# Five RMS-norm statistics taken off the matrix engine: turn, sum and spread through DRAM

## The chip, the cores and the metric

The kernel runs on one core of a Trainium2 chip. The metric is the device time of one execution in microseconds (us). The kernel before was timed three times: 2127.67, 2127.96 and 2129.14 us, median 2127.96 us. The trace is of one further, profiled execution.

## The reference

One layer of a streaming encoder on x of 1024 tokens by 1024 channels, all in f32: a SwiGLU feed-forward block, a token mixer (forgetting attention and top-k attention side by side) and a second SwiGLU block. Ahead of each stands an RMS norm over the channels, scaled and shifted by factors that come from a conditioning vector:

```python
def rms_norm(x, g):
    xf = x.astype(jnp.float32)
    y = xf * lax.rsqrt(jnp.mean(xf * xf, axis=-1, keepdims=True) + NORM_EPS)
    return (y * g.astype(jnp.float32)).astype(x.dtype)

def modulate(x, g, shift, scale):
    return rms_norm(x, g) * (1 + scale[:, None, :]) + shift[:, None, :]
...
h = modulate(x, norm_g[l, 0], mod[:, 0, 0], mod[:, 0, 1])
x = x + 0.5 * mod[:, 0, 2][:, None, :] * swiglu(h, ffn1_w1[l], ffn1_w3[l], ffn1_w2[l])
h = modulate(x, norm_g[l, 1], mod[:, 1, 0], mod[:, 1, 1])
y = hybrid_mixer(h, w_in[l], ...)
x = x + mod[:, 1, 2][:, None, :] * y
h = modulate(x, norm_g[l, 2], mod[:, 2, 0], mod[:, 2, 1])
x = x + 0.5 * mod[:, 2, 2][:, None, :] * swiglu(h, ffn2_w1[l], ffn2_w3[l], ffn2_w2[l])
```

Each token needs one number, the reciprocal root of the mean of its 1024 squares, and every channel of that token is multiplied by it.

## The kernel before

Activations lie transposed: x is eight tiles (one for each 128 channels, channel on the partition) by two halves of 512 tokens along the free side. A "half" below is 512 tokens. Three norms of two halves each make six norms. In the order of the kernel:

- the opening: the first half of the first norm. The work of the matrix engine (TensorE, PE in the profile) waits for it, and the change leaves it alone.
- norm A: the second half of the first norm, while PE works on products of the first half (`layer`, the second `sq = SquareSum`). Its factor goes into `Operands.second`, which scales the second half and forms the sums and differences that a Strassen-like scheme (`OPERANDS`, seven products for each pair of blocks) multiplies later.
- norm B: the first half of the second norm, inside the last passes of the first block's down-projection (`Down.run`, steps (5, 4) and (6, c)).
- norm C: the second half of the second norm, after the end of that down-projection. In between PE has only four projections of the first half, `first(0)` to `first(3)` (24 matmuls each, 128 x 432). Then the same projection runs over the second half, channel tile by channel tile, and needs norm C's factor for each of them (`norm_apply(k, 1, 1, ...)`, then `mm3` into four banks at once). Behind each `first(t)`, `natural` copies the bank to SBUF on ScalarE and stores it to DRAM (`d_na`).
- norm D: the first half of the third norm, inside `mixer_out`.
- norm E: the second half of the third norm, behind `mixer_out`, in the first steps of the second up-projection (`up_all`: twelve products of first-half operands come first, for three pairs of blocks).

Every norm has the same steps. `SquareSum.add` squares a tile on ScalarE (ACT) and adds it on VectorE (DVE) into one 128 x 512 accumulator, so that after eight tiles each partition holds a partial sum for each token. `norm_rms` sums over the partitions with four matmuls of the accumulator against a column of ones, one for each 128 tokens; `norm_root` turns the 128 x 4 result into reciprocal roots with twelve small DVE instructions; `norm_spread` puts them on all partitions with four matmuls of a broadcast column against the identity matrix. The result, `rb`, stays in a PSUM bank, from which DVE reads it as it scales the tiles (`Operands.scale`, `norm_apply`). Only norm E copies it from the bank to SBUF with ScalarE.

The order of instructions is planned before the kernel is built. `Plan` collects the tasks of a stage, and `flush` lists them for every engine by planned start time (`place`, `replay`, `dues`); the engines then run them in that order, each engine strictly in its own. All DMAs are issued from one queue, that of SyncE (SP), and one that has to wait holds back all behind it. The plan's price of a DMA is written in `place`:

```python
if e == "sync":
    self.wire = max(self.wire, s + 1.3) + t.bytes / 345e3
    end = self.wire + 1.7
```

Stages end at `nc.flush`. Opening, norm A and norm B lie in the first (up to the end of the first down-projection), norm C in the second, norms D and E in the last.

Of the kernel before, what the change touches and what calls it, by code (L numbers as in the profile page):

```python
# [10 lines left out]
F32 = mybir.dt.float32  # L11
# [15 lines left out]
H = 512  # L27
# [631 lines left out]
class SquareSum:  # L659


    def __init__(self, k, eng=None):
        self.k, self.acc, self.eng = k, None, eng or k.nc.gpsimd

    def add(self, x):
        nc = self.k.nc
        sq = t512(self.k, name="nsq" if self.acc else "nacc")
        nc.scalar.activation(sq, x, AF.Square)
        if self.acc:
            self.eng.tensor_add(self.acc, self.acc, sq)  # L670
        else:
            self.acc = sq

# [89 lines left out]
def t512(k, dt=F32, name="t", home="c"):  # L763

    p, tag, n = k.homes[home]
    return p.tile([128, H], dt, tag=tag, name=name, bufs=n)
# [1466 lines left out]
def layer(tc, xT, c, pos, ada_w, ada_b, ng, inv, w13a, w2a, w_a, w_f, w_q, w_g, fb, fg, dg, wbr, wout, w13b, w2b, out):  # L2233
    with ExitStack() as es:
# [45 lines left out]
        d_x = dram([8, 128, T], "d_x")  # L2280
        d_row = [[dram([1, H], f"d_row{i}{h}") for h in range(2)] for i in range(9)]
# [15 lines left out]
        with ExitStack() as ph:  # L2297
# [68 lines left out]
            def stats(j):  # L2366
                rms[j] = norm_rms(k, sq1[j].acc, rp, k.seeded if j == 0 else bank)

            def h0(cs):
                if cs[0] == 0:  # L2370
                    rms[0] = norm_spread(k, rms[0], bank)
                norm_apply(k, 1, 0, down.x, rms[0], cs)
# [28 lines left out]
            for i in range(8):  # L2401
                sq.add(x[i][0])
# [39 lines left out]
            rms[1] = norm_rms(k, sq.acc, rp, bank)  # L2442
            ops.rb[1] = norm_spread(k, rms[1], bank)
# [42 lines left out]
            nc.flush([t for r in down.x for t in r] + [t for r in wa for t in r] + k.hh[0] + k.hl[0] + [a.acc for a in sq1])  # L2486
# [17 lines left out]
            rb = norm_spread(k, rms[1], bank)  # L2504
# [133 lines left out]
        with ExitStack() as ph:  # L2638
# [25 lines left out]
            def stats(hf):  # L2664
                rms[hf] = norm_rms(k, sq[hf].acc, rp, bank)

            def spread(hf):
                ops.rb[hf] = norm_spread(k, rms[hf], bank)
                if hf:
                    t = t512(k, name="rb")  # L2670
                    nc.scalar.activation(t, ops.rb[hf], AF.Copy)
                    ops.rb[hf] = t
# [7 lines left out]
                10: [lambda: keep(0), lambda: spread(0)],  # L2680
                11: [lambda: more(0), pairs[0].load1], 12: [lambda: more(0), pairs[0].load2],
                13: [pairs[1].load1, lambda: pairs[0].sum32(nc.vector)], 14: [pairs[2].load1]}
            for n in range(9):
# [11 lines left out]
                   {1: [lambda: stats(1)], 3: [lambda: spread(1)], 4: [first1], 12: [next1], 14: [next1], 16: [next1],  # L2695
# [71 lines left out]
```

## Time and profile before

| | |
|---|---|
| median of three runs | 2127.96 us (2127.67 to 2129.14) |
| profiled execution, span from first to last instruction | 2126.6 us |
| PE matmuls busy | 2116.1 us (100% of the span) |
| PE weight loads busy | 1773.1 us (83%) |
| DVE busy | 1598.1 us (75%) |
| ACT busy | 1120.8 us (53%) |
| DMA, one queue | 216076 packets, 366.33 MB, 51.7% of 16 engines |

The profiled execution has no time of its own beside its span; the median of the runs is 1.4 us above that span, which is taken as what lies around it. Shares are over the whole span. Matmuls are pipelined, so each lasts longer in the trace (0.39 us) than the distance to the next (0.23 us), and the distance is what counts. "Idle before" and the name behind an arrow in a row tell what ended an engine's idle time.

### The profile page before, as it was taken

What the parts mean: (1) busy time and instruction counts of PE and PEld (TensorE: products, weight loads), DVE (VectorE), ACT (ScalarE), POOL (GpSimd) and SP (SyncE); (2) the same over time, 40 slices, a digit from 0 to 9 for tenths busy, and PEclk for the clock granted to TensorE, in tenths of its full rate; (3) what the DMA queues carried; (4) which work ended last, traced back from release to release, by engine and by line L of the source; (5) the groups of instructions that cost most, each with busy time, mean ns of one, the idle gap of its engine ahead of it and who ended that gap; (6) DMA issues with size and microseconds to landing.
All of it is one profiled execution on the core that took longest, in us unless ns stands there. A gap on an engine that the chain in (4) does not pass through costs nothing.

```text
span 2126.6 us, 31320 instructions
## 1 busy us (share of the span) xinstructions
PE 2116.1 (100%) x10632; PEld 1773.1 (83%) x10632; DVE 1598.1 (75%) x3079; ACT 1120.8 (53%) x2070; POOL 226.1 (11%) x231
## 2 busy tenths in 40 slices
PE   9999999999999999999999999999999999999999
PEld 7888888888888989998888777888888888888887
DVE  7987777879877399977886777698866755568665
ACT  4744444445456376886676777334543433334443
POOL 0001112200010110111442333000000000000000
PEclk9999999999999999999999999999999999999999
DMA  9446888899421444346453432896132533277521
GB/s 325 147 138 212 283 257 292 270 371 318 139 91 61 150 156 144 105 145 221 148 165 108 136 100 86 308 324 186 45 124 85 183 112 101 86 261 259 176 72 40
DMA packets 216237, 368.33 MB, mean 173 GB/s; under 512 B 29558, under 2 KB 67446, under 8 KB 216076
## 3 DMA queue, kind: packets, MB, share of 16 engines
q1 hardware_dynamic: 216076, 366.33, 51.7%
q8 instruction: 83, 1.36, 0.3%
q14 instruction: 78, 0.64, 0.1%
HBM read 268.99 MB, written 97.25 MB: 172 GB/s over the span
## 4 chain that ended last, share of the span: by engine, by line
PE 97%; DVE 2%; ACT 1%; issue 0%; DMA 0%; POOL 0%; SPq 0%; ACTq 0%; DVEq 0%; POOLq 0%
PE bs L606 38%; PE b L606 32%; PE pj L606 12%; PE py L606 8%; PE p L606 4%; PE pt L606 3%; DVE s L606 0%; DVE ptl L606 0%; DMA mraw<-in_ada_w 0%; ACT pth L606 0%; DVE qkv L606 0%; DVE pr L606 0%; ACT pr L606 0%; DVE qs L606 0%; DVE macc L606 0%
## 5 line engine op out<-in xcount | busy, mean ns | idle before, releaser
L606 PE MATMUL bs<-h,wh 128*128 128x512 f32 x1712 | 527.5, 390 | 1.1 <-ACT bs L606 0.7
L606 PEld LDWEIGHTS bs<-h,wh 128*128 128x128 f32 x1712 | 320.5, 188 | 70.0 <-ACT bs L606 1.6
L606 ACT ACTIVATE wh<-wr 128x512 fp32r<-128x512 f32 (+1 forms) x330 | 207.2, 638 | 295.4 <-PE bs L606 149.8
L606 PE MATMUL b<-h,wh 128*128 128x512 f32 x1072 | 332.5, 390 | 0.1
L606 PE MATMUL bs<-h,wl 128*128 128x512 f32 x856 | 331.6, 389 | 0.0
L606 DVE TENSOR_TENSOR wl<-wr,wh 128x512 fp32r<-128x512 f32 x306 | 211.4, 701 | 115.2 <-ACT wh L606 111.1
L606 PEld LDWEIGHTS b<-h,wh 128*128 128x128 f32 x1072 | 200.7, 188 | 43.2 <-ACT wh L606 0.5
L606 PE MATMUL b<-h,wl 128*128 128x512 f32 x536 | 208.3, 389 | 0.0
L606 PEld LDWEIGHTS bs<-h,wl 128*128 128x128 f32 x856 | 160.7, 188 | 33.6
L606 PE MATMUL pj<-wh,h 128*128 128x384 f32 (+1 forms) x768 | 178.4, 318 | 0.0
L606 ACT ACTIVATE wh<-a 128x512 fp32r<-128x512 f32 x132 | 83.4, 632 | 176.8 <-PE b L606 108.0
L606 DVE TENSOR_TENSOR wl<-a,wh 128x512 fp32r<-128x512 f32 x132 | 92.0, 698 | 81.9 <-ACT wh L606 79.7
L606 PE MATMUL b<-wh 128*128 128x512 f32 x360 | 138.7, 390 | 0.0
L606 PE MATMUL b<-wh,wl 128*128 128x512 f32 x352 | 136.7, 389 | 0.0
L606 PE MATMUL b<-wl,wh 128*128 128x512 f32 x352 | 136.7, 389 | 0.0
L606 PEld LDWEIGHTS pj<-wh,h 128*128 128x128 f32 x768 | 132.4, 189 | 0.3
L606 DVE TENSOR_TENSOR ptl<-pt,pth 128x512 fp32r<-128x512 f32 (+2 forms) x160 | 99.3, 634 | 41.0 <-ACT pth L606 40.2
L606 POOL TENSOR_SCALAR pr<-pr,mn 128x256 f32<-128x256 f32 (+7 forms) x128 | 102.1, 817 | 189.1 <-DVE mn L606 97.6
L606 PE MATMUL pj<-wl,h 128*128 128x384 f32 (+1 forms) x384 | 121.8, 318 | 0.0
L606 DVE TENSOR_TENSOR z<-bs,z 128x512 f32<-128x512 f32 x116 | 79.3, 687 | 56.3 <-PE bs L606 37.7
L606 PEld LDWEIGHTS b<-h,wl 128*128 128x128 f32 x536 | 100.6, 188 | 21.0
L606 ACT ACTIVATE pth<-pt 128x512 fp32r<-128x512 f32 (+2 forms) x160 | 87.0, 553 | 57.8 <-PE pt L606 56.2
(323 smaller groups left out, 4307.0 us busy)
## 6 DMA issues: line engine op xcount, KB each, us to landing
d_g<-z SPq DMA_DIRECT2D x154, 256.0 KB
g<-d_g SPq DMA_DIRECT2D x154, 256.0 KB
mraw<-in_ada_w SPq DMA_DIRECT2D x144, 256.0 KB
wr<-in_w13a SPq DMA_DIRECT2D x112, 256.0 KB
wr<-in_w13b SPq DMA_DIRECT2D x88, 256.0 KB
a<-in_w2a SPq DMA_DIRECT2D x44, 256.0 KB
a<-in_w2b SPq DMA_DIRECT2D x44, 256.0 KB
gw<-in_w_g SPq DMA_DIRECT2D x32, 256.0 KB
```

The costliest lines, as they stand in the source:

```text
L606: getattr(getattr(self.tc.nc, e), t.op)(*map(real, t.a), **{n: real(v) for n, v in t.kw.items()})
```

## The change

For norms A to E the partition sums and the spreading leave the matrix engine. The eighth addition of squares writes its result in another order of tokens (`turned`); DVE transposes it in blocks of 32 x 32 and sums groups of 32, which leaves, in each of four groups of 32 partitions, that group's partial sums of all 512 tokens. These 128 x 16 numbers are stored to DRAM (first transfer) and read back so that each partition has the four partial sums of four tokens (second transfer); DVE adds the four, and `norm_root` follows on 128 x 4 numbers as before. The roots are stored to DRAM as one row of 512 (third transfer) and read back to all 128 partitions as a 128 x 512 tile (fourth transfer). That tile in SBUF takes the place of the PSUM bank; norm E's copy on ScalarE goes. All four transfers are issued from SP. The accumulator tile and one more tile stay in use until then. The opening keeps its matmuls.

```diff
@@ class SquareSum
-    def add(self, x):
+    def add(self, x, turn=True):
         nc = self.k.nc
         sq = t512(self.k, name="nsq" if self.acc else "nacc")
         nc.scalar.activation(sq, x, AF.Square)
-        if self.acc:
+        self.n += 1
+        if self.n == 8 and turn:
+            self.turned = t512(self.k, name="nturn")
+            v = lambda t: t.rearrange("p (c b) -> p c b", b=16)
+            self.eng.tensor_add(self.turned.rearrange("p (b c) -> p c b", c=32), v(self.acc), v(sq))
+        elif self.acc:
             self.eng.tensor_add(self.acc, self.acc, sq)
         else:
             self.acc = sq
+
+
+def norm_far(k, sq, tmp, d):
+
+    nc = k.nc
+    a, t = sq.acc, sq.turned
+    nc.vector.transpose(a, t)
+    nc.vector.tensor_reduce(t[:, 0:16], a.rearrange("p (b r) -> p b r", r=32), axis=AX.X, op=ALU.add)
+    nc.sync.dma_start(d[0].rearrange("g (c b) -> (g c) b", b=16), t[:, 0:16])
+    four = a[:, 0:16].rearrange("p (g j) -> p g j", g=4)
+    nc.sync.dma_start(four, d[0].rearrange("g (p j) -> p g j", j=4))
+    v = tmp.tile([128, 4], F32, tag="nv", name="nv", bufs=2)
+    nc.vector.tensor_reduce(v, a[:, 0:16].rearrange("p (g j) -> p j g", g=4), axis=AX.X, op=ALU.add)
+    r = norm_root(k, v, tmp)
+    nc.sync.dma_start(d[1].rearrange("o (p j) -> p (o j)", j=4), r)
+    nc.sync.dma_start(t, d[1].to_broadcast([128, H]))
+    return t
...
+        d_n = [[dram([4, H], f"d_n{i}"), dram([1, H], f"d_r{i}")] for i in range(5)]
...
             def stats(j):
-                rms[j] = norm_rms(k, sq1[j].acc, rp, k.seeded if j == 0 else bank)
+                rms[j] = norm_far(k, sq1[j], rp, d_n[1 + j])
 
             def h0(cs):
-                if cs[0] == 0:
-                    rms[0] = norm_spread(k, rms[0], bank)
                 norm_apply(k, 1, 0, down.x, rms[0], cs)
...
             for i in range(8):
-                sq.add(x[i][0])
+                sq.add(x[i][0], False)
...
             for i in range(8):
                 sq.add(x[i][1])
-            rms[1] = norm_rms(k, sq.acc, rp, bank)
-            ops.rb[1] = norm_spread(k, rms[1], bank)
+            ops.rb[1] = norm_far(k, sq, rp, d_n[0])
...
             first(0)
             stats(1)
-            rb = norm_spread(k, rms[1], bank)
+            rb = rms[1]
             first(1)
...
             def stats(hf):
-                rms[hf] = norm_rms(k, sq[hf].acc, rp, bank)
-
-            def spread(hf):
-                ops.rb[hf] = norm_spread(k, rms[hf], bank)
-                if hf:
-                    t = t512(k, name="rb")
-                    nc.scalar.activation(t, ops.rb[hf], AF.Copy)
-                    ops.rb[hf] = t
+                ops.rb[hf] = norm_far(k, sq[hf], rp, d_n[3 + hf])
...
-                10: [lambda: keep(0), lambda: spread(0)],
+                10: [lambda: keep(0)],
...
-                   {1: [lambda: stats(1)], 3: [lambda: spread(1)], 4: [first1], 12: [next1], 14: [next1], 16: [next1],
+                   {1: [lambda: stats(1)], 4: [first1], 12: [next1], 14: [next1], 16: [next1],
```

## Rows read from the trace of the kernel before

**Rows 1.** The head of the profile's page and the matrix engine in its first part: busy time, share of the span, instructions.

```profile
span 2126.6 us, 31320 instructions
PE 2116.1 (100%) x10632; PEld 1773.1 (83%) x10632; DVE 1598.1 (75%) x3079; ACT 1120.8 (53%) x2070; POOL 226.1 (11%) x231
```

**Rows 2.** The list of instructions on the tile of the factors (nr), over the whole span: the spreading matmuls of all six norms.

```profile
L606 PE MATMUL b<-ident,nr x48: 271/275/362, 18.8 to 1499.9; 128*128 128x128 f32 x48
```

**Rows 3.** The timeline of PE around norm A (start us, length us, engine, line, operation, output and inputs, shape, count). Three matmuls of a group of three stand in two rows.

```profile
59.28 0.39 PE L606 MATMUL bs<-h,wl 128*128 128x512 f32 x1
...
60.19 0.95 PE L606 MATMUL b<-ones_col,nacc 128*128 128x1 f32 x8
61.00 0.72 PE L606 MATMUL bs<-h,wh 128*128 128x512 f32 x2
...
65.90 1.05 PE L606 MATMUL b<-ident,nr 128*128 128x128 f32 x8
66.71 0.71 PE L606 MATMUL bs<-h,wh 128*128 128x512 f32 x2
```

**Rows 4.** The timeline of PE around norm C: the four projections of the first half begin, the 96 matmuls of the second half begin, the next stage begins.

```profile
664.75 4.86 PE L606 MATMUL b<-wa,h 128*128 128x432 f32 x24
...
685.36 18.96 PE L606 MATMUL bs<-wa,h 128*128 128x432 f32 x96
704.16 0.63 PE L606 MATMUL pj<-h,wh 128*128 128x512 f32 x2
```

**Rows 5.** The timeline of DVE around norm C: the last addition of squares, the first and the last instruction of the root, the first scaling. In brackets the idle time before an instruction and what ended it.

```profile
666.57 0.69 DVE L606 TENSOR_TENSOR nacc<-nacc,nsq 128x512 f32<-128x512 f32 x1 [0.70 <-ACT nsq L606]
670.44 0.16 DVE L606 TENSOR_SCALAR nv<-b 128x4 f32<-128x4 f32 x1 [3.17 <-PE b L606]
...
672.62 0.16 DVE L606 SCALAR_TENSOR_TENSOR nr<-na,nr 128x4 f32<-128x4 f32 x1
674.20 3.68 DVE L606 TENSOR_TENSOR nt<-xc,b 128x512 f32<-128x512 f32 x6 [1.42 <-PE b L606]
```

**Rows 6.** The timeline of ACT in the same stretch: the copy of the first projection, and one channel tile's two steps between scaling and matmul.

```profile
669.65 0.53 ACT L606 ACTIVATE nat<-b 128x432 f32<-128x432 f32 x1 [3.11 <-PE b L606]
...
680.25 0.81 ACT L606 ACTIVATE nt<-nt,mod,A 128x512 f32<-128x512 f32 x1
...
681.37 0.62 ACT L606 ACTIVATE h<-nt 128x512 fp32r<-128x512 f32 x1
```

**Rows 7.** The timeline of the DMA queue of SP in the same stretch: the four stores of the projections, merged into one row from the first issue to the last.

```profile
670.21 16.38 SPq L606 DMA_DIRECT2D d_na<-nat  x4
```

**Rows 8.** The timeline of the first microseconds: a load of 4 KB and the first of eight loads of 256 KB are issued, and the two ACT instructions that wait for them start.

```profile
0.80 0.39 SPq L222 DMA_DIRECT2D cc<-in_c  x1
1.24 3.74 SPq L606 DMA_DIRECT2D x<-in_xT  x8
...
2.43 0.21 ACT L222 ACTIVATE cond<-cc 128x8 f32<-128x8 f32 x1 [0.35 <-DMA cc<-in_c]
4.20 0.63 ACT L606 ACTIVATE nacc<-x 128x512 f32<-128x512 f32 x1 [1.56 <-DMA x<-in_xT]
```

**Rows 9.** The timeline of SP at a quiet place: a row of 2 KB is stored to DRAM, and the load that reads it back is issued behind it.

```profile
1718.40 0.25 SPq L606 DMA_DIRECT2D d_row<-mrow  x1
1719.62 0.38 SPq L606 DMA_DIRECT2D mcol<-d_row  x1
```

**Rows 10.** The timelines of SP and DVE at a busy place: such a load is issued, and the instruction that waits for it starts.

```profile
424.50 0.37 SPq L606 DMA_DIRECT2D mcol<-d_row  x1
```

```profile
429.47 0.16 DVE L606 TENSOR_TENSOR mod<-mcol,ada_b 128x4 f32<-128x4 f32 x1 [3.76 <-DMA mcol<-d_row]
```

**Rows 11.** The groups of DVE instructions, shapes kept apart (count, busy us, mean ns of one, idle before): a sum over the free side, and the slowest form of 128 x 512 elements.

```profile
L606 DVE TENSOR_REDUCE fv<-fsq 128x8 f32<-128x512 f32 x24 | 16.4, 682 | 8.1 <-ACT fsq L606 8.0
...
L606 DVE TENSOR_TENSOR_SCAN tkg<-tktkj 128x512 f32<-128x512 bf16 x1 | 1.2, 1227 | 0.0
```

**Rows 12.** The DMA engines' busy share in the 40 slices (0.75 us each) of the stretch from 45 to 75 us.

```profile
DMA  9999999975888997899999999930000017000003
```

**Rows 13.** Busy time by engine in stretches of the kernel (stretch, its length, PE, weight loads, DVE, ACT, POOL, granted clock, DMA share, GB/s): behind norm A, and around norm D.

```profile
65.00:130.00 65.00, 65.00 (x292) 53.76 (x291) 62.47 (x105) 39.33 (x69) 0.00 (x0) 1.00 0.32 98
...
1400.00:1490.00 90.00, 90.00 (x406) 73.78 (x404) 81.75 (x145) 40.30 (x66) 0.00 (x0) 1.00 0.76 244
```

**Rows 14.** The timeline of DVE around norm A: the last addition of squares and the first use of the factor.

```profile
53.30 0.69 DVE L606 TENSOR_TENSOR nacc<-nacc,nsq 128x512 f32<-128x512 f32 x1
...
67.40 0.74 DVE L606 SCALAR_TENSOR_TENSOR x<-x,A,b 128x512 f32<-128x512 f32 x1
```

**Rows 15.** Norm B: the start of the root's first instruction (list of instructions on the tile nv), and the first use of the factor (timeline of DVE).

```profile
L606 DVE TENSOR_SCALAR nv<-bs x1: 162/162/162, 614.8 to 614.8; 128x4 f32<-128x4 f32 x1
```

```profile
639.46 0.68 DVE L606 TENSOR_TENSOR nt<-xc,b 128x512 f32<-128x512 f32 x1
```

**Rows 16.** The timeline of DVE around norms D and E: first use of norm D's factor and the last operand made from it; last addition of squares of norm E, first use of its factor.

```profile
1457.90 0.74 DVE L606 SCALAR_TENSOR_TENSOR xb<-xb,A,b 128x512 f32<-128x512 f32 x1
...
1475.37 0.74 DVE L606 SCALAR_TENSOR_TENSOR h<-xb,mod,h 128x512 fp32r<-128x512 f32 x1
...
1491.65 0.69 DVE L606 TENSOR_TENSOR nacc<-nacc,nsq 128x512 f32<-128x512 f32 x1
...
1500.83 2.08 DVE L606 SCALAR_TENSOR_TENSOR xb<-xb,A,rb 128x512 f32<-128x512 f32 x3 [0.39 <-ACT rb L606]
```

More of the change, by code (lines that the diff above doesn't have):

```diff
@@ L662, in __init__ @@
     def __init__(self, k, eng=None):
-        self.k, self.acc, self.eng = k, None, eng or k.nc.gpsimd
-    def add(self, x):
+        self.k, self.acc, self.eng, self.n, self.turned = k, None, eng or k.nc.gpsimd, 0, None
+    def add(self, x, turn=True):
         nc = self.k.nc
@@ L2485, in layer @@
             assert next(rest, None) is None and next(gw, 0) == 0
-            nc.flush([t for r in down.x for t in r] + [t for r in wa for t in r] + k.hh[0] + k.hl[0] + [a.acc for a in sq1])
+            nc.flush([t for r in down.x for t in r] + [t for r in wa for t in r] + k.hh[0] + k.hl[0] + [sq1[1].acc, sq1[1].turned])
             w0s.close()
```

## The prediction

> **What bounds the kernel now.** I read the page's first part, then the timeline of PE around each norm, then DVE, ACT and SP in the same stretches. Matmuls fill 2116.1 of 2126.6 us [rows 1], so there is no stall of note to remove: time can come only from matmuls that go, and can be lost only where PE has to wait for something new. The question is therefore twofold: how much PE time the ten groups of norm matmuls take, and whether the longer way through DRAM still ends before PE needs the result. The granted clock is 1.00 in the stretches that I looked at [rows 13].
>
> **What goes.** The spreading matmuls of six norms leave 48 records, eight for each [rows 2]; the summing ones look the same. Around norm A the sum starts at 60.19 and the next product at 61.00, so it takes 0.81 us of PE; the spread takes 66.71 - 65.90 = 0.81 [rows 3]. Something is lost behind each too: from 61.00 to 65.90 stand 21 matmuls, which at the distance before (59.28 to 60.19 are four, 0.2275 each) make 4.78 of the 4.90 us [rows 3]. So 0.93 for each group and 1.87 for a norm. Norm C confirms it from the outside: 96 matmuls of the second half take 704.16 - 685.36 = 18.80 us (0.196 each), the 96 of the first half with sum and spread between them 685.36 - 664.75 = 20.61, so 1.81 for the norm [rows 4]. Four norms at 1.87 and one at 1.81: **9.3 us** off PE, if nothing else happens. PSUM banks are also held for a shorter time; since PE waits for hardly anything today, I put that at nothing (half a us of gain at most, from the 10.5 us that PE is idle in all [rows 1]).
>
> **What is added, on one chain.** Between the last addition of squares and the first scaling come:
> - a transpose and a sum on DVE. The sum is 0.68 (128 x 512 to fewer, [rows 11]). No row shows a transpose, nor an addition that writes with a stride. Nearest are the addition itself, 0.69 [rows 5], and at the other end the slowest form of 128 x 512, 1.23 [rows 11]; a shorter one would only lengthen reserves and take nothing more off PE. I take 0.69 for both, so 1.4 for transpose and sum (1.9 at the upper end, and 0.5 more in the addition).
> - a small sum and the root: 672.62 + 0.16 - 670.44 = 2.34, and one more instruction of 0.2 [rows 5], so 2.5.
> - four transfers, each waiting for the one before. A 2 KB store was followed by the issue of its readback 1.22 later [rows 9]; a 4 KB load was used 1.63 after its issue and a 256 KB load 2.96 after [rows 8]. In that order, store, load, store, load: 1.22 + 1.63 + 1.22 + 2.96 = **7.0 us**, in a quiet queue. In a busy one the load of [rows 10] took 4.97. That load comes in 4-byte pieces, so its price may lie in the form and not in the load on the queue; the second transfer here has 512 pieces of 16 bytes, the first and third 128 pieces. I take the quiet prices for B to E and 5 us for the two early transfers of A; both ends go into the range.
>
> [...]
>
> Against this stands what goes from each chain: the two PE groups and the wait for them.
>
> **Where the chain ends, norm by norm.**
> *Norm C* is the tight one, as PE has nothing but four projections. Without norm matmuls they end at 664.75 + 96 x 0.196 = 683.6 [rows 4]. The squares are complete at 667.26; + 1.4 + 2.5 + 7.0 puts the factor at 678.2, and scaling, ACT's two steps and the first matmul 0.69 + 0.81 + 0.62 = 2.1 later [rows 5, 6]: 680.3, in time by 3.3. But SP also carries the four stores of the projections, in planned order. The plan prices every small transfer at 3.0 us (1.3 + 1.7 in `place`), so it expects the fourth transfer at 667.26 + 1.4 + 6.0 + 2.5 + 3.0 = 680.2. The third projection's store follows that projection's end by 670.21 - (664.75 + 24 x 0.196) = 0.76 [rows 4, 6, 7], so at 678.85 + 0.76 = 679.6: it is listed first, and the real fourth transfer, ready by 667.26 + 1.4 + 2.5 + 4.07 = 675.2, queues behind it until 680.0. Then + 2.96 + 2.1 = 685.1, a stall of 1.5, and somewhat more if the 216 KB ahead of it slow the load. I take **2.0** (0 if the order falls the other way, 3 at most).
> *Norm A*: squares complete at 53.99 [rows 14], + 1.4 + 10 (two transfers in a queue whose engines are busy until about 65 [rows 12]) + 2.5 + 1.22 + 2.96 = 72.1; the factor was first used at 67.40 [rows 14], so 4.7 late. DVE is the tight engine here, 62.47 of 65 us busy [rows 13], and gets 1.4 us more work, so a hole of up to 6.1 us. What covers it: PE has first-half products of six pairs, 24 of 12 matmuls, 65 us, and these began no earlier than 18.8 [rows 2], so it needs the second half at 86 or later, and the first group of operands takes DVE about 17 us from the first scaling (four times two scalings, three sums and a remainder, 0.7 each). That leaves 1.4 us or more, and DVE can split weights in the hole. I take **1.0** (0 to 4.7).
> *Norm E*: squares complete at 1492.34 [rows 16], + 10.9 = 1503.2, 2.4 later than 1500.83 [rows 16]. PE has twelve products of first-half operands (12 x 12 x 0.227 = 32.6 us) from the mixer's end, about 1490 (its last tile was squared and added by 1492.34), until 1522.6; 1503.2 + 17 is 1520.2. Nothing, with 2.4 in reserve.
> *Norm B* and *norm D* are idle in between anyway: B's root began at 614.8 and its factor was used at 639.46 [rows 15]; D's operands were ready at 1476.1, some 13 us before the mixer's end [rows 16]. Nothing.
> *DVE's added work* is 1.6 for a norm, 8 in all. It hides behind PE, except where DVE is nearly full, at A and around D (81.75 of 90 us [rows 13]): **0.8** for the stretch at D and the changed plan as a whole. SP gets 20 issues of 0.25 to 0.4 [rows 9], 7 us, hidden by its waits; ACT loses one copy, which shows nowhere.
>
> **Sum.** 9.3 - 2.0 - 1.0 - 0.8 = 5.5 us. The profiled execution would go from 2126.6 to 2121.1; the median stands 1.4 above that span, so **2122.5 us**, and 2120 to 2125 as this case's own range.
>
> **Rivals.**
> 1. *Everything is hidden.* The fourth transfer of C is listed ahead of the store, and A's hole is filled with splits. 2127.96 - 9.3 = 2118.7. For it: C's reserve of 3.3 us and the long covers of B, D and E. Against: the 3.0 us of the plan's price.
> 2. *The gain is given back.* A's hole comes through whole (4.7), C stalls 3, the full DVE costs 1.5: 9.2 of 9.3 us, 2127.9. For it: DVE's 62.47 of 65 us. Against: the order of DVE is planned by due times, so it has other work to take forward.
> 3. *Slower: small pieces are dear.* If the two transfers in small pieces that lie on the chain (the second and third) cost the 5 us of [rows 10] even in a quiet queue, the four make 14.2. C's reserve of 10.3 for them is then passed by 3.9; E comes 9.6 late with 4.8 covered, so 4.8; A ends 14.2 + 55.4 + 2.5 = 72.1, late as before, 4.7. Sum 13.4 - 9.3 = 4.1 slower, 2132.1. It decides from about 12.7 us for the four. For it: no row shows a quiet load in pieces this small. Against: the queue of [rows 10] carried other loads. [...]
>
> **Chances.** Forecast 0.45, rival 1 0.17, rival 2 0.25, rival 3 0.13. A measurement of this kernel can tell 0.2% (4.3 us) from no change, so faster means below 2123.7. Rival 1 and four fifths of the forecast's range lie there: 0.17 + 0.36 + 0.02 from rival 2's lower edge = 0.55. Slower is rival 3 and nothing else: 0.13. The rest, 0.32, is the same. The range of 2117 to 2131.5 leaves out rival 3's upper part and little below.
>
> **What would show it.** Right: no `ones_col` or `ident` matmuls after the opening; 192 matmuls of norm C's stretch in about 39.4 us again, less 1.8, plus a stall of some 2 us at the first second-half product; the fourth transfer issued just behind the third projection's store. Wrong: an idle PE around 98 us or 1523 us, a second transfer that takes over 3 us in a quiet queue, or a transpose well over 0.7 us.

## The result, and the profile after

The changed kernel takes 2141.41 us (median of 5 runs, 2138.78 to 2142.74) against 2127.96 (5 runs, 2127.67 to 2129.14). The ratio is 1.0059, 95% interval 1.0048 to 1.0069: 13.4 us slower, outside the range given. The profiled execution spans 2140.6 us, 14.0 more than [rows 1]. The head of its page and the engines' busy time:

```profile
span 2140.6 us, 31192 instructions
PE 2117.1 (99%) x10552; PEld 1767.3 (83%) x10552; DVE 1607.2 (75%) x3094; ACT 1122.0 (52%) x2069; POOL 225.2 (11%) x231
```

The 80 matmuls are gone (10632 to 10552), yet PE is busy 1.0 us longer and idle 23.5 us in place of 10.5. DVE has 9.1 us more work. So PE stands still in new places, and what it does takes longer somewhere. Where, the timeline of PE shows, around norms A, C and E; brackets hold the length of a stop ahead of the row and what ended it:

```profile
90.25 0.49 PE L606 MATMUL bs<-h,wh 128*128 128x512 f32 x1 [1.11 <-ACT h L606]
97.74 0.50 PE L606 MATMUL bs<-h,wh 128*128 128x512 f32 x1 [0.67 <-DVE h L606]
...
102.18 0.81 PE L606 MATMUL bs<-h,wh 128*128 128x512 f32 x2 [1.24 <-ACT bs L606]
...
670.75 18.96 PE L606 MATMUL b<-wa,h 128*128 128x432 f32 x96
691.70 20.62 PE L606 MATMUL bs<-wa,h 128*128 128x432 f32 x96 [1.98 <-ACT h L606]
712.16 0.64 PE L606 MATMUL pj<-h,wh 128*128 128x512 f32 x2
...
1523.94 0.50 PE L606 MATMUL bs<-h,wh 128*128 128x512 f32 x1 [1.10 <-ACT h L606]
1524.73 0.50 PE L606 MATMUL bs<-h,wh 128*128 128x512 f32 x1 [0.29 <-DVE h L606]
1526.09 0.80 PE L606 MATMUL bs<-h,wh 128*128 128x512 f32 x1 [0.62 <-ACT h L606]
1527.32 0.80 PE L606 MATMUL bs<-h,wh 128*128 128x512 f32 x1 [0.44 <-DVE h L606]
1529.94 0.80 PE L606 MATMUL bs<-h,wh 128*128 128x512 f32 x1 [1.40 <-ACT h L606]
```

Nearly all wait for operands of the second half, made from the late factor. At A the stops sum to 5.33 us (three that are not shown, of 0.62, 0.61 and 1.08, lie at 99, 100 and 119), at E to 3.85. One matmul there takes 0.50 up to 1525 and 0.80 from 1526 on, and at C, in the rows that answer to [rows 4], the 96 matmuls behind the stop need 20.62 in place of 18.96. The windows tell why: the last column but two, the granted clock, is 0.50 for some microseconds behind or among the stops at each of the three places.

```profile
65.00:130.00 65.00, 59.67 (x248) 46.70 (x247) 55.09 (x100) 35.53 (x62) 0.00 (x0) 0.97 0.35 106
102.69:106.10 3.41, 3.41 (x9) 2.65 (x9) 3.41 (x6) 3.41 (x7) 0.00 (x0) 0.50 0.68 250
693.19:696.60 3.41, 3.41 (x11) 3.13 (x10) 2.66 (x5) 3.31 (x6) 0.00 (x0) 0.50 0.05 19
1526.04:1532.87 6.83, 4.95 (x10) 3.04 (x11) 6.83 (x12) 2.87 (x5) 0.00 (x0) 0.50 0.00 0
```

The first row answers to [rows 13]: behind norm A not only PE fell (65.00 to 59.67) but also DVE, 62.47 to 55.09. In the stretch in which DVE was fullest it now has time to wait.

Milestones set against [rows 4] give the shares. The projections begin 6.0 late (670.75 to 664.75): A's loss less the gains of A and B. The next stage begins 8.0 late (712.16 to 704.16), so C adds 2.0 net. The other 6 come from the third norm's stretch (some 4) and from pieces between 712 and 1340 (some 2) that were not followed up.

At A, the timeline of SP shows how the four transfers got on (d_n, nacc<-d_n, d_r, nturn<-d_r):

```profile
65.14 0.33 SPq L606 DMA_DIRECT2D d_n<-nturn  x1
...
67.72 0.70 SPq L606 DMA_DIRECT2D nacc<-d_n  x1
...
73.15 1.36 SPq L606 DMA_DIRECT2D wr<-in_w13a  x3
74.60 0.38 SPq L606 DMA_DIRECT2D d_r<-nr  x1
75.04 1.85 SPq L606 DMA_DIRECT2D wr<-in_w13a  x4
78.18 0.33 SPq L606 DMA_DIRECT2D d_g<-z  x1
79.15 0.33 SPq L606 DMA_DIRECT2D nturn<-d_r  x1
```

And the timeline of DVE beside it, from the last addition of squares to the first use of the factor:

```profile
61.68 1.13 DVE L606 TENSOR_TENSOR nturn<-nacc,nsq 128x512 f32<-128x512 f32 x1
63.24 0.70 DVE L606 STREAM_TRANSPOSE nacc<-nturn 128x512 f32<-128x512 f32 x1
64.44 0.68 DVE L606 TENSOR_REDUCE nturn<-nacc 128x16 f32<-128x512 f32 x1
70.00 0.18 DVE L606 TENSOR_REDUCE nv<-nacc 128x4 f32<-128x16 f32 x1 [2.12 <-DMA nacc<-d_n]
84.89 2.08 DVE L606 SCALAR_TENSOR_TENSOR x<-x,A,nturn 128x512 f32<-128x512 f32 x3 [0.87 <-DMA nturn<-d_r]
```

The squares end at 62.8, not at 53.99 [rows 14], and the factor comes at 84.89, not at 67.40: 17.5 later.

### The profile page after: what moved, and what is told of

Read it like the earlier page. It is cut to its first block, busy times and chain, and to the rows that moved or that the text cites. A ratio compares the mean times of both kernels' runs of the same rounds, so it can differ in the third digit from the quotient of the medians.

```text
span 2140.6 us, 31192 instructions
## 1 busy us (share of the span) xinstructions
PE 2117.1 (99%) x10552; PEld 1767.3 (83%) x10552; DVE 1607.2 (75%) x3094; ACT 1122.0 (52%) x2069; POOL 225.2 (11%) x231
## 4 chain that ended last, share of the span: by engine, by line
PE 92%; DVE 4%; DMA 2%; ACT 1%; issue 1%; SPq 0%; POOL 0%; ACTq 0%; DVEq 0%; POOLq 0%
PE bs L606 36%; PE b L606 30%; PE pj L606 11%; PE py L606 8%; PE p L606 4%; PE pt L606 3%; DVE x L606 1%; DMA mraw<-in_ada_w 1%; DMA nturn<-d_r 0%; DVE h L606 0%; DVE s L606 0%; DMA na<-d_na 0%; DVE ptl L606 0%; DVE xb L606 0%; DMA x<-in_xT 0%
```

## The experiments

"Stop" is idle time of PE. Every comparison is with the kernel before, run beside it on the same chip; its median there was 2128.1 to 2128.6, and differences in us are taken from that median.

### One norm at a time

Each kernel takes the new way for some norms and has the old code for the others. For A alone, set against the changed kernel:

```diff
-                sq1[j].add(t)
+                sq1[j].add(t, False)
...
-                rms[j] = norm_far(k, sq1[j], rp, d_n[1 + j])
+                rms[j] = norm_rms(k, sq1[j].acc, rp, k.seeded if j == 0 else bank)
...
             def h0(cs):
+                if cs[0] == 0:
+                    rms[0] = norm_spread(k, rms[0], bank)
...
-            rb = rms[1]
+            rb = norm_spread(k, rms[1], bank)
...
-                sq[hf].add(x[i][hf])
+                sq[hf].add(x[i][hf], False)
...
-                ops.rb[hf] = norm_far(k, sq[hf], rp, d_n[3 + hf])
+                rms[hf] = norm_rms(k, sq[hf].acc, rp, bank)
```

B and D:

> Only the first halves of the second and third norms (B and D) by the new way; A, C and E stay on TensorE. Theory 1 (the loss comes from TensorE standing still at A, C and E, where the factor comes late, and from the half clock after each stop): B and D show no stop, so only their matmuls go, 2 x 1.87: 2124.2 us, 2122.5 to 2126. Theory 2 (the pieces are dear wherever they stand: strided additions, VectorE work and transfers cost about the same at each of the five, 13.4/5 = 2.7 each): 2133.3. Theory 3 (the plan of the order, drawn anew, costs the time): anything, and the parts don't add up.

Measured 2130.47, ratio 1.0009 (1.0000 to 1.0018). Every theory missed: neither the gain of theory 1 nor theory 2's 2133.3. The trace's largest new stop:

```profile
1514.18 0.51 PE L606 MATMUL bs<-h,wl 128*128 128x512 f32 x1 [2.38 <-DVE wl L606]
```

It lies in the third norm's stretch, at E's place, though E is on TensorE here. Two smaller ones (1.19 at 24, 1.08 at 779) lie far from B and D. `wl` is one of the two parts into which a weight tile is split before PE multiplies it; ACT makes `wh`, DVE makes `wl`.

A alone:

> Only the second half of the first norm (A) by the new way. Theory 1: about 9.9 of stops and slow clock behind 90 us, less 1.9 of matmuls: 2136.0 us, 2134 to 2138, with idle PE at 90 to 120 us. Theory 2: 2130.7. Theory 3: as above; the sum of the four kernels of this call would differ from the whole change's +13.4 by over 5.

Measured 2134.78, ratio 1.0032 (1.0019 to 1.0044): +6.4, stops as in the whole change. Theory 1.

C alone:

> Only the second half of the second norm (C) by the new way. Theory 1: a stop of 2.0 and 1.7 more by the slow clock behind it, less 1.8 of matmuls: 2129.8 us, 2128.5 to 2131; 96 matmuls of the second half in about 20.6 us against 18.96. Theory 2: 2130.7 with the stretch behind the norm unchanged. Theory 3: as above.

Measured 2130.16, ratio 1.0007 (0.9998 to 1.0016): +1.8, and in the profiled execution the stop of 1.98. But there the 96 matmuls behind it took 19.08 us, with no half clock. The eleven executions tell more: in five the mean granted clock was 1.000 and the time 2128.2 to 2129.6, in six it was 0.999 and the time 2130.2 to 2131.8, 2.0 more on the mean. So a stop of 1.98 has the half clock behind it in some executions (0.50 for 3.41 us in the profile of the whole change) and not in others (1.00 in this one).

D and E:

> Both halves of the third norm (D and E) by the new way, the others on TensorE. Theory 1: D gains 1.9, E loses 7.3 of stops and slow clock at 1523 to 1533 less 1.9: 2131.6 us, 2130 to 2133.5. Theory 2: 2133.3, spread over the stretch. Theory 3: as above.

Measured 2132.81, ratio 1.0021 (1.0012 to 1.0030): +4.4.

B alone and D alone, run later to part the first of these:

> Only B by the new way. B and D together came out 1.9 slower than before, and their trace has one stop of 2.38 at 1514 with half clock behind it, in the stretch of the third norm. If that stop comes from D alone (the third norm's stretch is planned anew where D goes through DRAM), B alone gains its matmuls: 2126.5 us, 2125.5 to 2127.5, and no new stop. If B costs something of its own: 2128 or more.

Measured 2126.64, ratio 0.9993 (0.9984 to 1.0002): -1.4, near the 1.87 of its matmuls, though the interval just reaches no change. There is no new stop at B or in the third norm's stretch. The eleven executions spread from 2125.5 to 2129.2, all at a mean clock of 1.000; the profiled one is the slowest, with stops of 1.09 and 0.99 in the opening (at 12 and 34) that the profile of before has not. So not all spread between executions comes from the clock.

> Only D by the new way. If D's new plan of the third norm's stretch costs what separates B with D from B alone (a stop of 2.4 at 1514 and half clock, less 1.9): 2131.5 us, 2129.5 to 2133, with that stop in the trace. If B and D cost only together: 2126.5.

Measured 2131.37, ratio 1.0012 (1.0003 to 1.0021): +2.8, with the same stop of 2.38 (at 1513.85). So D costs, and B doesn't. Two windows of before:

```profile
1440.00:1475.00 35.00, 35.00 (x163) 29.20 (x163) 29.75 (x59) 16.50 (x27) 0.00 (x0) 1.00 0.67 196
1505.00:1520.00 15.00, 15.00 (x68) 12.40 (x67) 15.00 (x25) 8.53 (x14) 0.00 (x0) 1.00 0.05 18
```

and of D alone:

```profile
1440.00:1475.00 35.00, 35.00 (x156) 28.97 (x156) 25.30 (x52) 14.53 (x23) 0.00 (x0) 1.00 0.58 180
1505.00:1520.00 15.00, 12.62 (x48) 9.75 (x47) 14.95 (x25) 7.86 (x13) 0.00 (x0) 0.89 0.01 2
```

DVE (third pair of numbers) works 14.95 of 15 us while PE stops, but it was as full there in before, without a stop. The difference lies ahead: D's factor was first used at 1466.91, 9 us later than in before (1457.90 [rows 16]), and between 1440 and 1475 DVE did 4.4 us less work. By 1520 it had caught up (68.19 us of work since 1440, 68.51 in before), while PE, with two groups of matmuls less, reached the mixer's end 2.8 us earlier (1487.21, in before 1490.00). PE came early to a stretch in which DVE is the one that is full. That reading fits the rows; that the redrawn order has no part in the 2.38 is not shown.

E was not run by itself; next to D's 2.8, the 4.4 of D and E leave 1.6 for it. A, B, C and D with E add up to 6.4 - 1.4 + 1.8 + 4.4 = 11.2 of the 13.4. Theory 2 is out (the norms differ in sign), and so is theory 3 in its strong form: the parts nearly add up. The 2.2 that are left are about as much as the medians spread.

### Norm C: two chains that end together

The prediction had a stop of 2.0 at C, from the fourth transfer behind a store in SP's queue. The stop came, at 1.98, and the fourth transfer did stand behind that store. So: order it ahead. `nc.gate` is a list of instructions behind which the plan has to put what follows on the same queue; the order of PE and ACT stays as in C alone.

```diff
             rb = rms[1]
+            nc.gate = [len(nc.tasks) - 1]
             first(1)
             first(2)
             first(3)
+            nc.gate = []
```

> C by the new way, and the stores of the second to fourth projection put behind the fourth transfer in SP's queue; nothing else changes its order. Theory 1 (the fourth transfer stands in SP's queue behind a store that waits for PE, 3.2 us): its issue comes about 1.4 behind the third's, at about 683 of C's trace, nt about 3 earlier, no stop at 686 and no half clock: 2126.5 us, 2125.5 to 2127.5. Rival (the transfers' own latency makes the stop): a stop of over 1 stays, 2129 to 2130.

Measured 2129.67, ratio 1.0006 (0.9997 to 1.0015). The rival's number, but not for its reason. The first scaling, from the timeline of DVE:

```profile
681.45 2.50 DVE L606 TENSOR_TENSOR nt<-xc,nturn 128x512 f32<-128x512 f32 x4 [5.43 <-DMA nturn<-d_r]
```

Counted from the start of the projections (664.18 here, 665.51 in C alone), that is 17.3 in place of 18.7: the factor did come 1.4 earlier. The stop is 1.98 as before. The timeline of ACT has the reason:

```profile
678.48 0.53 ACT L606 ACTIVATE nat<-b 128x432 f32<-128x432 f32 x1 [4.17 <-PE b L606]
683.18 0.53 ACT L606 ACTIVATE nat<-b 128x432 f32<-128x432 f32 x1 [4.17 <-PE b L606]
683.61 0.80 ACT L606 ACTIVATE nt<-nt,mod,A 128x512 f32<-128x512 f32 x1
684.44 0.63 ACT L606 ACTIVATE h<-nt 128x512 fp32r<-128x512 f32 x1
```

The copy of the fourth projection waits for that projection, and the first operand's two steps stand behind it on ACT. PE can't have an operand earlier than its own last projection plus copy and two steps: 0.53 + 0.80 + 0.63 = 1.96. In before ACT did those steps first and the copy at 685.73. In C alone the factor was used at 684.17, and 2.1 for scaling and ACT's steps make 686.3, where PE went on at 686.45: the queue on SP by itself would have made nearly the same stop. Two chains ended within 0.3 us of each other, and taking away this one shows nothing; the other was not taken away by itself. So both:

```diff
             def first(tk):
                 ps = bank()
                 proj_n(k, ps[:, :NA], wa, NA, tk)
-                natural(tk, ps)
+                if tk < 3:
+                    natural(tk, ps)
+                return ps
...
-            first(3)
-            nc.gate = []
+            last = first(3)
+            gate, nc.gate = nc.gate, []
...
                 norm_apply(k, 1, 1, down.x, rb, [c])
+                if c == 1:
+                    nc.gate = gate + [t.i for t in nc.tasks[-4:] if t.engine == "scalar"]
+                    natural(3, last)
+                    nc.gate = []
```

> C with the held stores of the experiment before, and besides it the copy of the fourth projection (nat) put on ACT behind the operands of the first two channel tiles. In C alone all four copies stand on ACT ahead of the first operand, the fourth waits for the fourth projection's end, and the factor came 0.3 us before that: two chains that end together. Theory (both held the second half; taking away one shows nothing): with both gone the first operand is ready about 0.5 behind the fourth projection's end; stop at most 0.6, no half clock: 2126.8 us, 2125.8 to 2127.8. Rival (there is a third): the stop of 1.98 stays, 2129.7.

Measured 2128.67, ratio 0.9998 (0.9989 to 1.0007): +0.3 where the held stores alone had +1.6, and 0.9 above the range expected. No execution has a mean clock of 0.999, yet they spread from 2126.4 to 2129.5. In the profiled one, the fastest of the eleven, the stop was 0.91:

```profile
683.35 19.07 PE L606 MATMUL bs<-wa,h 128*128 128x432 f32 x96 [0.91 <-ACT h L606]
```

and there the transfers are what ends late. The profile bears the mechanism out; its gain in time was smaller than expected, and how long the stop was in the slower executions is not known.

### The half clock by itself

C alone again, with eight matmuls between projections and second half that nobody needs:

```diff
             first(3)
+            idle = bank()
+            for _ in range(8):
+                nc.tensor.matmul(idle[:, :NA], k.hh[0][0][:, 0:128], wa[0][0], start=True, stop=True)
             ps = [k.seeded() for _ in range(4)]
```

> C by the new way, and eight matmuls more (of operands at hand, into a bank that nobody reads) between the fourth projection and the second half's 96, 1.6 us of PE time; the stop of 1.98 shrinks to 0.4. Theory 1 (a stop of 2 us halves PE's clock for 3.41 us in some executions and not in others, 1.7 each time): the end comes no later in any execution and the slow ones vanish: 2128.6 us, all within about 2127.5 to 2129.7. Rival (the spread of C's runs, 2128.2 to 2131.8, has another cause): the spread and the median of 2130.2 stay, or the filling adds to it.

Measured 2128.91, ratio 1.0004 (0.9995 to 1.0012), all eleven executions within 2128.1 to 2129.7 and at a clock of 1.000. The stop is 0.57 and the second half runs at its full rate:

```profile
665.46 20.53 PE L606 MATMUL b<-wa,h 128*128 128x432 f32 x104
686.56 19.07 PE L606 MATMUL bs<-wa,h 128*128 128x432 f32 x96 [0.57 <-ACT h L606]
```

Work without use halved the loss (+1.8 to +0.9; the intervals overlap, the clearer sign is that no execution was slow). The half clock came with a stop of 1.98 and not with one of 0.57, and it is a cost of its own: 20.62 us for the 96 matmuls in the whole change, 19.07 here. The line by the mean clock is less clean elsewhere: with the held stores (a stop of 1.98 too) four of eleven executions were at 0.999, and two of the seven at 1.000 took 2129.8 and 2130.4.

### Norm A: what is lost is VectorE's time

First try: let the chain start earlier.

```diff
+            nc.behind = -60
             for i in range(8):
                 load_x(x[i][1], i, 1)
+            nc.behind = 0
...
             sq = SquareSum(k, nc.vector)
+            nc.behind = -60
             for i in range(8):
                 sq.add(x[i][1])
             ops.rb[1] = norm_far(k, sq, rp, d_n[0])
+            nc.behind = 0
```

> A by the new way, with the loads of x's second half, its squares and the norm ranked 60 instructions earlier in the plan: the four transfers then stand together in SP's queue, ahead of ten weight loads and with two stores of d_g between. Theory 1 (A's factor is late, at 84.9, because the transfers wait in SP's queue among weight loads and land behind them): factor at 75 to 79, the stops at 90 to 103 and the half clock gone or under 2 in all: 2127.5 us, 2126 to 2130. Rival (the added VectorE work, or the four latencies alone, make A late): 2133 or more.

Measured 2141.44, ratio 1.0061 (1.0048 to 1.0073): +13.4 for A alone, twice as bad. Yet the factor was used at 79.67, 6 earlier than in A alone (85.6). So a late factor is not what is lost. Ten weight loads now stood behind the fourth transfer, at 76 to 82, and DVE had neither factor nor weights: it worked 9.82 us between 65 and 85, about as little as in A alone. That makes no more than A alone's loss; the stops at A grew from 5.0 to 6.5 us, and others came with the redrawn order (1.26 at 243). Why the loss doubled stays open. The windows of before (the third pair of numbers is DVE):

```profile
65.00:85.00 20.00, 20.00 (x94) 16.69 (x93) 19.89 (x35) 12.91 (x22) 0.00 (x0) 1.00 0.11 42
85.00:110.00 25.00, 25.00 (x112) 20.56 (x111) 25.00 (x42) 16.78 (x30) 0.00 (x0) 1.00 0.41 127
```

of A alone:

```profile
65.00:85.00 20.00, 20.00 (x90) 16.54 (x90) 9.46 (x27) 6.86 (x12) 0.00 (x0) 1.00 0.59 174
85.00:110.00 25.00, 20.20 (x71) 14.62 (x70) 25.00 (x42) 17.30 (x30) 0.00 (x0) 0.86 0.23 73
```

Before, DVE had 44.9 us of work in 45. In A alone it stands idle for 10.5 of the first 20 while the transfers travel; PE still has first-half products there, and runs out in the next 25, in which DVE has no pause.

If that is it, other work for DVE during the wait should help although the factor stays late. The kernel moves sixteen loads and the differences made of them (`sum32`) ahead of the norm and holds the first transfer behind the loads:

```diff
-            ops.rb[1] = norm_far(k, sq, rp, d_n[0])
+            n = len(nc.tasks)
+            for i in range(2, head):
+                pairs[i].load1("c", (1,))
+            pairs[0].load1()
+            pairs[0].load2()
+            nf = [t.i for t in nc.tasks[n:] if t.engine == "sync"]
+            pairs[0].sum32(nc.vector)
+            ops.rb[1] = norm_far(k, sq, rp, d_n[0], nf)
```

> A by the new way, with the loads of sixteen weight tiles and two sums over them emitted ahead of the norm, and the first of the four transfers held behind those loads in SP's queue: VectorE has splits and sums to do while the transfers travel. Theory (A costs what VectorE stands idle while it waits, 9.8 of 20 us at 65 to 85, in a stretch in which it had 54.8 of 55 us of work before): VectorE busy 14 or more of the 20 us, and the loss of 6.5 shrinks by as much as the idle time does: 2130 us, 2127.5 to 2132.5. Rival (PE waits because the factor itself is late, whatever VectorE does meanwhile): 2134 or more with a factor as late as 80 to 85.

Measured 2132.28, ratio 1.0016 (1.0007 to 1.0025). The factor is used at 84.1, as late as before, DVE works 16.77 of the 20 us, and 2.5 of the 6.4 us are back:

```profile
65.00:85.00 20.00, 20.00 (x90) 16.57 (x89) 16.77 (x37) 10.33 (x19) 0.00 (x0) 1.00 0.27 74
85.00:110.00 25.00, 22.86 (x91) 17.71 (x91) 25.00 (x41) 18.00 (x32) 0.00 (x0) 0.93 0.41 127
```

The loss shrank by less than DVE's idle time did (7.3), so that time is not the whole of it. And the other way round, the kernel before with DVE burdened and no transfer; the plan is untouched, some splits are only issued three times:

```diff
+            for t in [t for t in nc.tasks[m:] if t.op == "tensor_sub" and t.kw == {} and t.a[0].tile.kw.get("tag") == "wl"][8:15]:
+                t.times = 3
```

> The kernel before, with no transfer and the factor on time; seven splits of weights (wl) behind A's factor are done three times over, about 9 us more of VectorE's time between 64 and 98, in the same order of everything. Theory (A's loss is VectorE's time, of which there is none to spare in that stretch): stops at 85 to 120 as in A alone, 4 to 5 and half clock with them: 2135 us, 2132 to 2138. Rival (a late factor costs, VectorE's time doesn't): 2130.5 or less.

The trace shows four splits tripled and not seven (3087 DVE instructions in place of 3079), at 65, 70, 74 and 78, of which the first row is one; each takes 2.14 us in place of 0.69, so DVE got 5.8 us more work. Measured 2134.62, ratio 1.0030 (1.0018 to 1.0042): +6.0, as much as A. The two large stops:

```profile
64.74 2.15 DVE L606 TENSOR_TENSOR wl<-wr,wh 128x512 fp32r<-128x512 f32 x3
```

```profile
67.41 1.16 PE L606 MATMUL b<-ident,nr 128*128 128x128 f32 x8 [1.11 <-DVE nr L606]
...
103.11 1.22 PE L606 MATMUL bs<-h,wh 128*128 128x512 f32 x2 [2.10 <-ACT bs L606]
```

The first is the root's, which the first tripled split delays, so the factor was not quite on time: first use at 69.09, 1.7 later than [rows 14]. The second comes where DVE has no pause (25.00 of 25 us from 85 to 110), with half clock behind it. So 5.8 us of more work for DVE cost 6.0, and some 10 us of idling in the same stretch cost 6.4: DVE's time is lost either way, and most of it is paid only at 90 to 120.

### Norm E: longer shown, shorter not

D by the new way, E's sums too, but E's factor spread by PE:

```diff
     r = norm_root(k, v, tmp)
+    if not far:
+        return r
...
+            def spread():
+                t = t512(k, name="rb")
+                nc.scalar.activation(t, norm_spread(k, ops.rb[1], bank), AF.Copy)
+                ops.rb[1] = t
```

> D by the new way; E with its sums the new way (turned, summed, two transfers) and its factor spread by TensorE and copied by ACT as before: the third and fourth transfer of E fall away, the VectorE work stays. Theory (E's stops, 4.2 and 3.4 by the half clock, come from the transfers' latency: the factor of D and E's run was ready 5.8 after the root): factor 3 to 4 us earlier, stops and half clock down to 2 in all: 2128.3 us, 2126.5 to 2130.5. Rival (the added VectorE work in a stretch where VectorE is full makes E late): 2132 or more.

In this kernel E's columns get one another's factors (the root holds four neighbours in a partition, the spreading takes them 128 apart); number and size of the instructions are unaffected. Measured 2143.21, ratio 1.0066 (1.0053 to 1.0079): worse than everything expected, and inconclusive, because the plan of the whole last stretch came out another way. The largest stop lies 160 us ahead of E:

```profile
1338.20 1.22 PE L606 MATMUL b<-h,wh 128*128 128x512 f32 x2 [4.89 <-ACT wh L606]
```

So from here on with the order of every queue kept. First, 16 columns in place of 512 in the last transfer of A and E:

```diff
-    nc.sync.dma_start(t, d[1].to_broadcast([128, H]))
+    n = 16 if other else H
+    nc.sync.dma_start(t[:, 0:n], d[1][:, 0:n].to_broadcast([128, n]))
+    nc.tasks[-1].bytes = 4 * 128 * H
```

> The whole change; the last transfer of A and of E brings 16 columns of the factor to each partition and not 512 (the other columns are multiplied by what stands there: left out), and the order of every queue is kept. Theory (the stops come from the transfers' latency): the factor comes 2 to 3 earlier at A and at E, the stops shrink by as much and some half clock goes: 2136 us, 2133.5 to 2138.5. Rival (the plan's order and the added VectorE work make the stops): 2140 or more, stops as before.

Measured 2140.90, ratio 1.0053 (1.0039 to 1.0067), the rival's number; but the factor was not used 2 to 3 earlier. From issue to use passed 3.45 us in place of 4.39 at E, 5.50 in place of 5.74 at A. These are upper bounds for the small load, since DVE came to it without a pause, from a split:

```profile
1516.93 0.69 DVE L606 TENSOR_TENSOR wl<-wr,wh 128x512 fp32r<-128x512 f32 x1 [2.03 <-ACT wh L606]
1517.54 1.41 DVE L606 SCALAR_TENSOR_TENSOR xb<-xb,A,nturn 128x512 f32<-128x512 f32 x2
```

How long the small load itself took is not shown, so the theory was not put to the full test. The run tells something all the same. At E the factor was used 0.9 earlier, and PE's first stop was 1.11, as in the whole change. The timeline of ACT there:

```profile
1521.71 0.63 ACT L606 ACTIVATE wh<-wr 128x512 fp32r<-128x512 f32 x1 [0.72 <-PE b L606]
1522.24 0.70 ACT L606 ACTIVATE h<-t,mod 128x512 fp32r<-128x512 f32 x1
```

The first operand stands on ACT behind a split of weights that waits for PE, as at C: again a second chain with the same end.

Then the same transfer issued twice:

```diff
     nc.sync.dma_start(t, d[1].to_broadcast([128, H]))
+    nc.tasks[-1].times = 2 if other else 1
```

> The whole change; the last transfer of A and of E is issued twice, one behind the other, with the order of all else kept. Theory: the factor comes 3.5 to 5.5 later at A and at E, and each of these costs as much or more: 2150 us, 2147 to 2154. Rival: 2143 or less.

Measured 2149.78, ratio 1.0099 (1.0085 to 1.0113): +21.2, where the whole change had +13.4, so 7.7 more. At A the factor came 2.8 later (87.65); at E it came 21.5 behind the last addition of squares in place of 18.65, so 2.9 later. PE's first stop at E:

```profile
1528.99 0.79 PE L606 MATMUL bs<-h,wh 128*128 128x512 f32 x1 [3.51 <-ACT h L606]
```

The two delays of 5.7 cost 7.7, and the half clock grew with them. The whole change had 0.50 for 6.83 us at E and for 3.41 at A. Here single matmuls take 0.79 or 0.80 us in place of 0.50, and those in a row come 0.42 apart in place of 0.23, from 1529.0 to about 1538.6 at E, and at A from 93.0 to 98.3 and again from 106.6 to 112.2; the mean clock of the profiled execution is 0.994, in the whole change 0.997. Later cost more here than it was late; 0.9 earlier at E gained nothing, since ACT's order held the same place. DVE idles at E as it does at A: in the changed kernel it works 8.15 us between 1505 and 1520, while the transfers travel, and 14.59 in the next 15, in which PE stops. How E's own loss divides between those, and how much of it the transfers' latency alone would make, stays open.

### What can be kept

> B as it is, C with the held stores and the held copy; A, D and E on TensorE. If the two gains add up (B measured 1.4, C expected 1.3): 2125.3 us, 2124 to 2126.7. If C's chain still ends late, 2128.

Measured 2125.36 (11 runs, 2124.33 to 2126.37), ratio 0.9987 (0.9978 to 0.9996): 3.0 faster than before and faster than both kernels. That is the expected sum, but not the sum of the parts as measured (-1.4 for B, +0.3 for C with both held): the two gain 1.9 more together. In the profiled execution, again the fastest of the eleven, C's factor was used 16.2 us behind the start of the projections, where C with both held had 17.6; why it came earlier is not shown. At C there is no stop left:

```profile
662.48 18.96 PE L606 MATMUL b<-wa,h 128*128 128x432 f32 x96
681.28 18.96 PE L606 MATMUL bs<-wa,h 128*128 128x432 f32 x96
```

## Why the prediction was wrong, step by step

The forecast was 5.5 us faster, the measurement 13.4 slower: 18.9 apart. By the kernels of single norms (forecast and measured, each with its matmuls): A -0.9 and +6.4; D with E -2.9 and +4.4; C +0.2 and +1.8; B -1.9 and -1.4. So A and the third norm miss by 7.3 each, C by 1.6, B by 0.5; 2.2 belong to no norm. No rival had it either: the only one that pointed to slower, rival 3, did so for a reason that did not come about.

- **What goes, 9.3 us: right.** The 80 matmuls went, and B alone gained 1.4 of its 1.87. In the last kernel the 192 matmuls of C's stretch end at 681.28 + 18.96 - 662.48 = 37.8, where before took 39.4 [rows 4].
- **Durations of the pieces: right on DVE, too small for the transfers.** The transpose took 0.70 (0.69 taken). The addition that writes with a stride took 1.13, not 0.69: inside the bound of 1.23. The store's readback was issued 1.41 later (1.22 taken), the small load was used 2.06 after its issue at C (1.63 taken), and the last load took 3.4 to 4.4 in a quiet queue where 2.96 was taken: 8.3 to 9.3 for the four in place of 7.0. Rival 3 is out in its own form: the small pieces were not dear (2.06, not 5).
- **Norm C, 2.0: right size, one of two causes, and a term missing.** The stop was 1.98. The queue on SP was as foretold, with the fourth transfer just behind the third projection's store, but undoing it left the stop where it was. "Then + 2.96 + 2.1 = 685.1" took ACT as free for the first operand, and the plan had put the fourth projection's copy ahead of it, which makes the same stop. That the size came out is therefore in part luck. The half clock, 1.7 us (20.62 in place of 18.96) in about half of the executions (six of eleven of C alone), was not in the sum at all.
- **Norm A, 1.0: a large error.** Three steps failed together. "Squares complete at 53.99" took the start from a plan that was going to be redrawn; they were complete at 62.8. The chain behind them was summed to 18.1 us and took 22.1, not where the 10 us stood (the first two transfers took 4.9) but in the third and fourth, which were priced as quiet, 4.2, and took 10.3 among the weight loads in SP's queue. So the factor came at 84.89 and not at 72.1, and the first-half products, which lasted until 89.1, no longer covered it. And "DVE can split weights in the hole": it couldn't, since the weights' loads stood among and behind the transfers. The prediction named DVE as the tight engine and a hole of up to 6.1; the hole was 10, and 1.0 was taken for it because PE's cover was counted to the first group of operands and not through the backlog behind it. ("86 or later" and "1.4 us or more" are loose as well: 18.8 + 65 makes 84, and 72.1 + 17 makes 89.1, so the prediction's own figures leave nothing in reserve.) A alone cost 6.4 net.
- **Norm E, nothing: wrong.** Two terms of the reserve were off. From complete squares to the first use passed 17.5 us (1501.90 to 1519.42) where 10.9 were taken: beside the last load, the small sum of the readback stood on DVE behind splits and a sum that waited for PE, 4.9 behind the load's issue. And of the twelve first-half products nine were left at the mixer's end: they covered 24.6 us (1498.2 to 1522.8), not 32.6.
- **Norm D, nothing: wrong in sign.** D's own chain was covered, as foretold. Its price of 2.8 arises some 45 us behind the factor's first use, where DVE is full (14.95 of 15 us) and PE isn't what is short: fewer matmuls gained nothing there. The 0.8 taken for DVE's work "at D and the changed plan as a whole" is the term: with its 1.87 of matmuls, D alone cost 4.6.
- **Norm B: right.** Rival 2 had the right direction for A and C and for DVE; it ended at no change because it, too, had no half clock and no loss at D and E.
- **The signs.** Of those named for a wrong prediction, PE did stand idle around 98 and 1523 us; no transpose was slow, and where DVE did not hold back its use (at C) the second transfer took 2.06, not 3.

## What to carry to other kernels

Before work is moved off PE, list in every stretch which engine has no pause, and count its idle time as lost even when PE is covered at that moment: at A DVE stood idle at 65 to 85 us, and PE paid for it from 90 on. Where an operand is late, look for all chains that end at the same place (the transfer, and what stands ahead of the consumer on its own engine, as the copy of 0.53 us ahead of the first operand on ACT did at C), for undoing one showed nothing there: the stop stayed at 1.98. Price a stop of PE with the half clock behind it (up to 1.7 us behind one of 1.98 here), and change such things norm by norm: of the five, B gained, C came out about even by itself once both its chains were undone, A and D lost, and E, never run alone, lost beside D.

## What the runs showed of the hardware

The granted clock went to 0.50 behind stops of PE: for 3.41 us at A and at C and for 6.83 at E in the whole change, for 3.41 at C with the held stores. A stop of 1.98 did it in some executions and not in others: the 96 matmuls behind it took 20.62 us in the profile of the whole change and 20.60 in that of the held stores, but 19.08 in that of C alone. Single stops of about 1.0, as the one of 1.01 at 777 in before, did not (granted clock 1.00 from 765 to 790); a stop of 2.38 did, in B and D as in D alone (0.89 over 1505 to 1520). Several short ones did as well: at A in the whole change 1.11, 0.67, 0.62, 0.61 and 1.24 us, within 13 us, with the 0.50 behind the last. What sets the length, and why the same stop does it in one execution and not in the next, is not shown.

A load of one DRAM row to all 128 partitions was used 4.39 us after its issue with 512 columns (norm E of the whole change) and at most 3.45 after with 16; the bytes of the 512 were moving until some 4.0 us behind the issue. What part of that goes with the size is not shown.
